# Moving GpSimd's two-input element-wise work to VectorE in a one-core diffusion-transformer kernel

## The chip, the cores and the metric

The kernel runs on one core of one Trainium2 chip. The metric is the device time of one execution in microseconds (us). The core's engines are named as the profile names them: PE (TensorE, matmuls), DVE (VectorE), ACT (ScalarE), POOL (GpSimd) and SP (SyncE, which issues the weight loads). Each engine runs its own queue in order; an instruction whose inputs are not ready holds up what stands behind it on the same engine.

## The reference, cut to what matters

Two blocks work on a latent sequence x of 256 tokens and a context sequence of 256 tokens, both 1024 wide, in float32. The first block has two layers, each a modulated SwiGLU feed-forward, a mixer, and a second feed-forward, with an RMS norm ahead of each:

```python
x = x + 0.5 * mx[:, 2] * swiglu(ada_norm(x, norm_g[l, 0], mx[:, 0], mx[:, 1]), ffn_w_in[l, 0], ffn_w_out[l, 0])
hx = ada_norm(x, norm_g[l, 1], mx[:, 3], mx[:, 4])
# l == 0: even_mixer (differential attention with 2-D rotation, and a bidirectional mLSTM)
# l == 1: odd_mixer (bidirectional gated linear attention)
x = x + mx[:, 5] * yx
x = x + 0.5 * mx[:, 8] * swiglu(ada_norm(x, norm_g[l, 2], mx[:, 6], mx[:, 7]), ffn_w_in[l, 1], ffn_w_out[l, 1])
...
return rms_norm(x, final_g)
```

The second block has two layers of a mixer (latent attention, then neighbourhood attention) and a squared-ReLU MLP, each closed by a layer norm:

```python
h = x * (1 + sc1) + sh1
x = _layer_norm(alpha * x + g1 * y, ln1_g[i], ln1_b[i])
x = _layer_norm(alpha * x + g2 * _mlp(x * (1 + sc2) + sh2, mlp_w1[i], mlp_w2[i]), ln2_g[i], ln2_b[i])
```

## The kernel before

**Tiling.** The activations stay in SBUF, transposed, as `xT`: 8 pieces `k` of 128 channels by 512 tokens, the context (CTX) in columns 0 to 255 and the latent (X) in 256 to 511. Every product of weights and activations is a sum of three matmuls on split numbers (`mm3`): high part by high part (L291), weight high by activation low (L292), weight low by activation high (L293). PE therefore needs a low part of every weight and of every activation.

**Weights.** SP loads a chunk of 128 by 1024 (tile `wraw`, 5 buffers), ACT copies it to the high part (L221, tile `whl`, 4 buffers), and `split_lo` subtracts it from the raw chunk, which gives the low part (L229). Which engine runs L229 stands in `R["lo"]`, set by `lo_on`: VectorE as a rule, and GpSimd (or the two in turn) at the seams between two parts, while the latent MLP's middle runs, and, by the `lo` items, inside the even attention.

**Seams.** Between two parts, `boundary` runs the old part's last output matmuls, the norm and the new part's first matmuls, in a mixture that should keep PE at work. DVE adds each output to `xT` (L811 for an RMS seam, L824 for a layer-norm one), gathers sums (L556, L558), turns PE's token sums into an inverse root by a chain of instructions on two numbers (L526 to L530; for a layer norm also L691 to L696), and writes it on a diagonal (L570). PE spreads the result over the partitions (L571), and DVE then applies the norm for each piece k: L617 and L619 (RMS), or L743, L744, L752 and the low part L753 (layer norm). Before L571 there are no statistics, so nothing of the new part's products can start. At the seam into the last MLP the latent is led instead: L651 and L652 write the scaled, not yet normalised activations, PE multiplies 258 columns of them, and the norm is put in afterwards (L767, L768).

**Attention.** The even attention rotates heads: `stream_shuffle` (L1116), a product with the cosines (DVE) and one with the sines (L1118, POOL), then their sum (L1119). Its steps and those of the gated linear attention run under `in_order`, which binds PE, DVE and ACT, but not POOL, to the order in which the program emits their instructions. Everywhere else a scheduler orders each engine's queue by priorities.

**Other lines of GpSimd.** L686 (low part of the modulated activations, even k), L753 (six of eight k, `LN_LO`), L1705 (two long subtractions for each direction of the gated linear attention), L802 (four additions in the last norm), and memsets and triangular masks.

Of the kernel before, what the change touches and what calls it, by code (L numbers as in the profile page):

```python
# [56 lines left out]
LN_T = ()  # L57
LN_LO = (0, 1, 2, 4, 5, 6)
TMP_BUFS = 9
# [33 lines left out]
def build(nc, tc, ctx, A, stop=None):  # L93
# [9 lines left out]
    V, ACT, PE, G = nc.vector, nc.scalar, nc.tensor, nc.gpsimd  # L103
    POOL = (G,)
    AFTER = (G,)
    EV_LO = (G,)
    RMS_LOS = (G,)
    FN_LOS = (V, G)
    LN_LOS = (G,)
    FULL, CTX, X = slice(0, 512), slice(0, 256), slice(256, 512)  # L110
# [89 lines left out]
    def run_items():  # L200
# [23 lines left out]

        def split_lo(eng=None):
            raw, n, hl = chunks[ws[st["split"]]]
            if eng is None:
                eng = R["lo"][st["split"] % len(R["lo"])]
            eng.tensor_tensor(hl[:, 1, 0:n], raw[:, 0:n], f32(hl[:, 0, 0:n]), ALU.subtract)  # L229
            st["raw"] -= 1  # L230
            st["split"] += 1
            load()
# [23 lines left out]
        for it in items:  # L256
# [13 lines left out]
            elif it[0] == "lo":  # L270
                if half:
                    split_lo(*it[1:])
            elif it[0] == "f":
# [40 lines left out]

    R = {"lo": (V,)}

    def lo_on(*engines):

        R["lo"] = engines

# [357 lines left out]
    def modulate(h, li, shift, scale, s, ks):  # L678
        seg = SEGS[s]
        for k in ks:  # L680
# [4 lines left out]
            V.tensor_scalar(t, x, a, b, ALU.mult, ALU.add)  # L685
            (V if k % 2 else G).tensor_tensor(h.at(1, k, seg), t, f32(h.at(0, k, seg)), ALU.subtract)  # L686

# [11 lines left out]
    class LayerNorm:  # L699
# [39 lines left out]
        def apply(self, s, ks):  # L739
            seg, bc = SEGS[s], self.bc[s]  # L740
            for k in ks:
# [3 lines left out]
                if self.li is not None:  # L745
# [5 lines left out]
                    else:  # L751
                        V.tensor_scalar(t, x, a, b, ALU.mult, ALU.add)  # L752
                    (G if k in LN_LO else V).tensor_tensor(h.at(1, k, seg), t, f32(h.at(0, k, seg)), ALU.subtract)  # L753
            for k in ks:
# [193 lines left out]
    def boundary(exits, norm, entries, e_segs, n_segs, after=()):  # L948
# [10 lines left out]
        if entries and tuple(n_segs) == (1,):  # L959
# [25 lines left out]
            items.extend(("w1", k) for k in keys)  # L985
            do(lo_on, *AFTER)
            do(end_lead, norm)
# [7 lines left out]
        EX = LN_EX if ln else RMS_EX  # L995
        if entries:
            do(lo_on, *(LN_LOS if ln else FN_LOS if isinstance(norm, FinalNorm) else RMS_LOS))
        for u in exits:
# [34 lines left out]
        else:  # L1033
            run_entries(entries, {EN[0]: [soon(norm.stats, 1)], EN[1]: [soon(norm.spread, 1), apply(1, range(8))]})
        do(lo_on, V)


    class Ffn:
# [54 lines left out]
        def middle(self, n_hid, n_out):  # L1093
            for g in range(3):
                for q, u in enumerate(self.hid[g]):
                    if g == 0 and q < (2 if self.seg is FULL else 4):
                        continue
                    body([u], self.seg, n_hid)
                do(lo_on, V)
                do(self.swap)  # L1100
# [6 lines left out]
    def rope(ps, dst, seg):  # L1107
# [4 lines left out]
        if seg.stop == 512:  # L1112
            p = ps[:, 256 - o:512 - o]
            t = tt()
            sh, t1 = t[:, 0:256], t[:, 256:512]
            V.stream_shuffle(sh, p, [(i + 16) % 32 for i in range(32)])  # L1116
            V.tensor_tensor(t1, p, cosT, ALU.mult)
            G.tensor_tensor(sh, sh, sinT, ALU.mult)  # L1118
            V.tensor_tensor(dst[:, X], t1, sh, ALU.add)  # L1119
# [56 lines left out]
    class Even:  # L1176
# [390 lines left out]
        def middle(self):  # L1567
# [49 lines left out]
            def steps():  # L1617
                more(EV_N[0])
                for step in range(21):
# [10 lines left out]
                    if step < 16:  # L1630
                        items.append(("lo", EV_LO[step % len(EV_LO)]))
                    if step in merges:
# [20 lines left out]
    class Odd:  # L1653
# [46 lines left out]
        def decay_log(self, d):  # L1700
# [3 lines left out]
            for o in range(0, 2048, 1024):  # L1704
                G.tensor_tensor(la[:, o:o + 1024], la[:, o:o + 1024], a[:, o:o + 1024], ALU.subtract)  # L1705
            if d:
# [309 lines left out]
    class Out2:  # L2016
# [19 lines left out]
        def middle(self, done=0):  # L2036
            body(self.u[done:3], self.seg)
            if self.seg is X:
                do(lo_on, *POOL)
            body(self.u[3:4], self.seg, hooks={CK: [lambda: center(self.seg, self.rest)]})  # L2040
# [173 lines left out]
    class Mlp:  # L2214
# [39 lines left out]
        def middle(self, n_ada):  # L2254
            for g in range(4):
                for u in self.hid[g][0 if g else 4 if self.seg is FULL else 5:]:
                    body([u], self.seg, n_ada)
                do(lo_on, V)
                do(self.swap)
# [10 lines left out]
    class Na:  # L2270
# [97 lines left out]
        def middle(self):  # L2368
# [17 lines left out]
            def ahead(step):  # L2386
                if 28 <= step < 32:
                    items.extend([("hi",), ("lo", G)])

# [211 lines left out]
```

## Time and profile before

| | |
|---|---|
| median of 3 runs | 2836.68 us (2833.68 to 2838.6) |
| the profiled execution | 2832.91 us |
| its span, first to last instruction | 2831.2 us |
| busy: PE, DVE, ACT, POOL | 2734.7, 2000.6, 1112.1, 240.8 us |
| mean granted TensorE clock | 0.988 |

The span is what the profile shows; the 1.7 us around it are not in any row. A busy figure sums the durations of an engine's instructions; an instruction that stands still while it holds its engine is counted as busy, so a busy DVE is not DVE at work all the time.

### The profile page before, as it was taken

What the parts mean: (1) busy time and instruction counts of PE and PEld (TensorE: products, weight loads), DVE (VectorE), ACT (ScalarE), POOL (GpSimd) and SP (SyncE); (2) the same over time, 40 slices, a digit from 0 to 9 for tenths busy, and PEclk for the clock granted to TensorE, in tenths of its full rate; (3) what the DMA queues carried; (4) which work ended last, traced back from release to release, by engine and by line L of the source; (5) the groups of instructions that cost most, each with busy time, mean ns of one, the idle gap of its engine ahead of it and who ended that gap; (6) DMA issues with size and microseconds to landing.
All of it is one profiled execution on the core that took longest, in us unless ns stands there. A gap on an engine that the chain in (4) does not pass through costs nothing. (4 is left out here: it accounts for less than half of the span.)

```text
span 2831.2 us, 41057 instructions
## 1 busy us (share of the span) xinstructions
PE 2734.7 (97%) x15940; PEld 2363.8 (83%) x15940; DVE 2000.6 (71%) x3817; ACT 1112.1 (39%) x1955; POOL 240.8 (9%) x184
## 2 busy tenths in 40 slices
PE   7999999999999999999999999999999999998998
PEld 4888888878888888888889999976888888976898
DVE  4877786566888787886764755744898857447766
ACT  3222235653222233222264644454443323535544
POOL 0000010221000010000120010200200002003200
PEclk8999999999999999999999999999999999999999
DMA  6656542111566544665542355430165542313453
GB/s 254 203 197 208 179 141 89 48 53 60 191 209 217 170 158 160 214 214 172 170 157 78 113 186 181 133 96 1 60 196 190 180 141 82 121 64 116 144 183 105
DMA packets 114068, 413.15 MB, mean 146 GB/s; under 512 B 12496, under 2 KB 14800, under 8 KB 112336
## 3 DMA queue, kind: packets, MB, share of 16 engines
q1 hardware_dynamic: 112256, 407.64, 44.1%
q10 hardware_dynamic: 1616, 2.88, 0.3%
q8 instruction: 125, 2.05, 0.3%
q14 instruction: 71, 0.58, 0.1%
HBM read 409.42 MB, written 1.05 MB: 145 GB/s over the span
## 5 line engine op out<-in xcount | busy, mean ns | idle before, releaser
L292 PE MATMUL p<-slot,whl 128*128 128x512 f32 (+2 forms) x4256 | 1445.0, 340 | 15.5 <-DVE slot L652 6.1
L291 PE MATMUL p<-slot,whl 128*128 128x512 f32 (+2 forms) x4256 | 1446.0, 342 | 6.8 <-ACT slot L618 2.9
L293 PE MATMUL p<-slot,whl 128*128 128x512 f32 (+2 forms) x4256 | 1441.3, 340 | 6.7 <-DVE whl L229 5.0
L292 PEld LDWEIGHTS p<-slot,whl 128*128 128x128 f32 x4256 | 811.1, 191 | 111.0 <-DVE slot L652 7.1
L291 PEld LDWEIGHTS p<-slot,whl 128*128 128x128 f32 x4256 | 808.0, 191 | 106.0 <-issue 8.6
L293 PEld LDWEIGHTS p<-slot,whl 128*128 128x128 f32 x4256 | 810.9, 191 | 96.0 <-DVE whl L229 5.7
L221 ACT ACTIVATE whl<-wraw 128x1024 fp32r<-128x1024 f32 (+1 forms) x527 | 542.8, 1043 | 510.8 <-PE p L293 290.9
L229 DVE TENSOR_TENSOR whl<-wraw,whl 128x1024 fp32r<-128x1024 f32 (+1 forms) x460 | 560.8, 1221 | 198.8 <-ACT whl L221 190.9
L396 DVE SCALAR_TENSOR_TENSOR t<-wraw,sB 128x1024 bf16<-128x1024 f32 x448 | 534.5, 1218 | 1.8 <-ACT sB L150 1.8
L229 POOL TENSOR_TENSOR whl<-wraw,whl 128x1024 fp32r<-128x1024 f32 (+1 forms) x67 | 167.0, 2499 | 2050.6 <-ACT whl L221 2025.1
L1069 ACT ACTIVATE t<-p 128x512 f32<-128x512 f32 (+1 forms) x86 | 47.1, 548 | 539.5 <-PE p L293 539.5
L1071 DVE TENSOR_TENSOR t<-t,p 128x512 f32<-128x512 f32 (+1 forms) x86 | 53.8, 626 | 218.4 <-PE p L293 161.4
L291 PE MATMUL p<-whl,slot 128*128 128x256 f32 (+1 forms) x432 | 126.3, 292 | 0.0
L292 PE MATMUL p<-whl,slot 128*128 128x256 f32 (+1 forms) x432 | 124.3, 288 | 1.8 <-DVE whl L229 1.8
L293 PE MATMUL p<-whl,slot 128*128 128x256 f32 (+1 forms) x432 | 124.0, 287 | 0.0
L811 DVE SCALAR_TENSOR_TENSOR xT<-p,mod,xT 128x256 f32<-128x256 f32 x192 | 85.8, 477 | 32.3 <-PE p L293 32.1
L590 DVE TENSOR_TENSOR slot<-t,slot 128x512 fp32r<-128x512 f32 (+1 forms) x166 | 101.4, 616 | 3.4 <-ACT slot L589 3.0
L589 ACT ACTIVATE slot<-t 128x512 fp32r<-128x512 f32 (+1 forms) x166 | 89.3, 542 | 18.7 <-DVE t L2239 7.3
L824 DVE SCALAR_TENSOR_TENSOR xT<-p,mod,xT 128x256 f32<-128x256 f32 x119 | 54.3, 478 | 48.9 <-PE p L293 48.5
L556 DVE TENSOR_TENSOR t<-t 128x256 f32<-128x256 f32 (+1 forms) x98 | 74.6, 762 | 19.5 <-ACT t L555 18.4
L291 PEld LDWEIGHTS p<-whl,slot 128*128 128x128 f32 x432 | 83.0, 192 | 4.0 <-issue 2.3
L292 PEld LDWEIGHTS p<-whl,slot 128*128 128x128 f32 x432 | 83.0, 192 | 3.3 <-DVE whl L229 2.2
(314 smaller groups left out, 1959.4 us busy)
## 6 DMA issues: line engine op xcount, KB each, us to landing
wraw<-in_ada SPq DMA_DIRECT2D x224, 512.0 KB, 4.1
wraw<-in_ffn_in SPq DMA_DIRECT2D x176, 512.0 KB, 4.4
wraw<-in_mlp SPq DMA_DIRECT2D x128, 512.0 KB, 3.5
wraw<-in_ffn_out SPq DMA_DIRECT2D x64, 512.0 KB, 4.3
wraw<-in_ffn_out SPq DMA_DIRECT2D x32, 384.0 KB, 3.7
slot<-in_ada SPq DMA_DIRECT2D x8, 1024.0 KB, 16.2
wraw<-in_even_a SPq DMA_DIRECT2D x16, 512.0 KB, 3.5
wraw<-in_odd_a SPq DMA_DIRECT2D x16, 512.0 KB, 3.6
```

What stands on the lines that cost most here:

```text
L221: ACT.activation(out=hl[:, 0, 0:n], in_=raw[:, 0:n], func=AF.Copy)
L229: eng.tensor_tensor(hl[:, 1, 0:n], raw[:, 0:n], f32(hl[:, 0, 0:n]), ALU.subtract)
L291: PE.matmul(ps, w[0], a[0], start=first, stop=False)
L292: PE.matmul(ps, w[0], a[1], start=False, stop=False)
L293: R["pe"] = PE.matmul(ps, w[1], a[0], start=False, stop=last).ins
L396: V.scalar_tensor_tensor(j.bitcast(BF16)[:, 0:1024], raw, 1.0, sB[:, r, :], ALU.mult, ALU.mult, accum_out=mods[li][:, f, r:r + 1])
L556: V.tensor_tensor(a, a, sq[:, seg], ALU.add)
L589: ACT.activation(out=hi, in_=src, func=AF.Copy)
L590: (eng or V).tensor_tensor(lo, src, f32(hi), ALU.subtract)
L811: V.scalar_tensor_tensor(xT[:, m, SEGS[s]], ps[:, q - seg.start:q - seg.start + 256], mod(li, gate)[:, m, s:s + 1], xT[:, m, SEGS[s]], ALU ...
L824: V.scalar_tensor_tensor(xT[:, m, SEGS[s]], ps[:, q - seg.start:q - seg.start + 256], mod(li, gate)[:, m, s:s + 1], xT[:, m, SEGS[s]], ALU ...
L1071: V.tensor_tensor(sa[:, 0:w], sa[:, 0:w], pb, ALU.mult)
```

## The change

All the switches by which an engine is chosen go (`lo_on`, `R["lo"]`, `LN_LO` and the tuples of engines), and five lines always use VectorE:

```diff
-        def split_lo(eng=None):
+        def split_lo():
             raw, n, hl = chunks[ws[st["split"]]]
-            if eng is None:
-                eng = R["lo"][st["split"] % len(R["lo"])]
-            eng.tensor_tensor(hl[:, 1, 0:n], raw[:, 0:n], f32(hl[:, 0, 0:n]), ALU.subtract)
+            V.tensor_tensor(hl[:, 1, 0:n], raw[:, 0:n], f32(hl[:, 0, 0:n]), ALU.subtract)
...
-            (V if k % 2 else G).tensor_tensor(h.at(1, k, seg), t, f32(h.at(0, k, seg)), ALU.subtract)
+            V.tensor_tensor(h.at(1, k, seg), t, f32(h.at(0, k, seg)), ALU.subtract)
...
-                    (G if k in LN_LO else V).tensor_tensor(h.at(1, k, seg), t, f32(h.at(0, k, seg)), ALU.subtract)
+                    V.tensor_tensor(h.at(1, k, seg), t, f32(h.at(0, k, seg)), ALU.subtract)
...
-        if entries:
-            do(lo_on, *(LN_LOS if ln else FN_LOS if isinstance(norm, FinalNorm) else RMS_LOS))
...
-            G.tensor_tensor(sh, sh, sinT, ALU.mult)
+            V.tensor_tensor(sh, sh, sinT, ALU.mult)
...
-                        items.append(("lo", EV_LO[step % len(EV_LO)]))
+                        items.append(("lo",))
...
-                G.tensor_tensor(la[:, o:o + 1024], la[:, o:o + 1024], a[:, o:o + 1024], ALU.subtract)
+                V.tensor_tensor(la[:, o:o + 1024], la[:, o:o + 1024], a[:, o:o + 1024], ALU.subtract)
...
-            if self.seg is X:
-                do(lo_on, *POOL)
```

Of POOL's instructions 122 move: 67 of L229, 30 of L753, 13 of L1118, 8 of L686 and 4 of L1705. The memsets, the masks and the four additions of L802 stay. No DMA is changed, and no matmul is added or removed. The scheduler is given other instructions, so the queues of DVE, ACT and PE shift a little as well.

The rows below are DVE's queue; a number behind a name is that of the buffer or bank. In the changed file the lines stand lower: L220 is the weight's low part (L229 before), L543 and L545 are the sums L556 and L558, L515 to L517 the inverse root's L528 to L530, L557 the diagonal L570, L639 the led low part L652, L678 to L683 the statistics L691 to L696, L730 and L731 the applied norm L743 and L744, L739 and L740 the L752 and L753, and L811 the addition L824.

The first place is the seam from the latent attention into the first MLP, on DVE, where the context's norm is applied (k = 2 to 4) and the latent's statistics begin; before:

```order
L558 TENSOR_TENSOR t_17499<-t_17499,xT_81 128x256
L743 TENSOR_TENSOR xT_81<-xT_81,p_17842 128x256
L753 TENSOR_TENSOR slot_17664<-t_17871,slot_17662 128x256
L744 TENSOR_TENSOR xT_81<-xT_81,p_17842 128x256
L743 TENSOR_TENSOR xT_81<-xT_81,p_17842 128x256
L556 TENSOR_TENSOR t_17500<-t_17500,t_17881 128x256
L752 TENSOR_SCALAR t_17931<-xT_81,mod2_89 128x256
L556 TENSOR_TENSOR t_17500<-t_17500,t_17921 128x256
L744 TENSOR_TENSOR xT_81<-xT_81,p_17842 128x256
L691 TENSOR_SCALAR tiny_18002<-p_17997 128x2
```

and after, at the same place on DVE:

```order
L545 TENSOR_TENSOR t_17499<-t_17499,xT_81 128x256
L740 TENSOR_TENSOR slot_17664<-t_17871,slot_17662 128x256
L543 TENSOR_TENSOR t_17500<-t_17500,t_17881 128x256
L220 TENSOR_TENSOR whl_17889<-wraw_17556,whl_17889 128x1024
L811 SCALAR_TENSOR_TENSOR xT_81<-p_17894,mod2_89,xT_81 128x256
L220 TENSOR_TENSOR whl_17924<-wraw_17614,whl_17924 128x1024
L545 TENSOR_TENSOR t_17499<-t_17499,xT_81 128x256
L543 TENSOR_TENSOR t_17500<-t_17500,t_17921 128x256
L730 TENSOR_TENSOR xT_81<-xT_81,p_17842 128x256
L678 TENSOR_SCALAR tiny_18002<-p_17997 128x2
```

Two subtractions of weights (L220) now stand between the fourth and the fifth piece of the context, ahead of the sums that the latent's statistics need. A third stands between the diagonal (L557) and the first L730 of this seam, and none between the context's token sums and L557.

The second place is the seam into the last MLP, on DVE, where the last outputs come in (L824) and the led low parts (L652) are written; before:

```order
L824 SCALAR_TENSOR_TENSOR xT_81<-p_22853,mod3_90,xT_81 128x256
L652 SCALAR_TENSOR_TENSOR slot_22974<-xT_81,mod3_90,slot_22972 128x256
L558 TENSOR_TENSOR t_22748<-t_22748,xT_81 128x256
L556 TENSOR_TENSOR t_22749<-t_22749,t_22880 128x256
L652 SCALAR_TENSOR_TENSOR slot_22974<-xT_81,mod3_90,slot_22972 128x256 x2
L824 SCALAR_TENSOR_TENSOR xT_81<-p_22888,mod3_90,xT_81 128x256
L652 SCALAR_TENSOR_TENSOR slot_22974<-xT_81,mod3_90,slot_22972 128x256
L558 TENSOR_TENSOR t_22748<-t_22748,xT_81 128x256
```

and after, at the same place on DVE:

```order
L811 SCALAR_TENSOR_TENSOR xT_81<-p_22853,mod3_90,xT_81 128x256
L220 TENSOR_TENSOR whl_22883<-wraw_22653,whl_22883 128x1024
L545 TENSOR_TENSOR t_22748<-t_22748,xT_81 128x256
L543 TENSOR_TENSOR t_22749<-t_22749,t_22880 128x256
L811 SCALAR_TENSOR_TENSOR xT_81<-p_22888,mod3_90,xT_81 128x256
L220 TENSOR_TENSOR whl_22918<-wraw_22758,whl_22918 128x1024
L545 TENSOR_TENSOR t_22748<-t_22748,xT_81 128x256
L543 TENSOR_TENSOR t_22749<-t_22749,t_22915 128x256
L220 TENSOR_TENSOR whl_22953<-wraw_22763,whl_22953 128x1024
L811 SCALAR_TENSOR_TENSOR xT_81<-p_22923,mod3_90,xT_81 128x256
L639 SCALAR_TENSOR_TENSOR slot_22974<-xT_81,mod3_90,slot_22972 128x256
```

Three subtractions of weights have come in between the additions, and the led low parts are pushed behind them.

The third place is the chain of statistics of that same seam on DVE, a few rows on; before:

```order
L652 SCALAR_TENSOR_TENSOR slot_22975<-xT_81,mod3_90,slot_22973 128x256
L691 TENSOR_SCALAR tiny_23070<-p_23065 128x2
L692 TENSOR_SCALAR tiny_23071<-p_23065 128x2
L693 TENSOR_TENSOR tiny_23072<-tiny_23070 128x2
L694 TENSOR_TENSOR tiny_23071<-tiny_23071,tiny_23072 128x2
L526 TENSOR_SCALAR tiny_23073<-tiny_23071 128x2
L528 TENSOR_TENSOR tiny_23078<-tiny_23073 128x2
L529 SCALAR_TENSOR_TENSOR tiny_23079<-tiny_23078,tiny_23071 128x2
```

and after:

```order
L639 SCALAR_TENSOR_TENSOR slot_22975<-xT_81,mod3_90,slot_22973 128x256
L220 TENSOR_TENSOR whl_23035<-wraw_22851,whl_23035 128x1024
L678 TENSOR_SCALAR tiny_23070<-p_23065 128x2
L679 TENSOR_SCALAR tiny_23071<-p_23065 128x2
L680 TENSOR_TENSOR tiny_23072<-tiny_23070 128x2
L681 TENSOR_TENSOR tiny_23071<-tiny_23071,tiny_23072 128x2
L220 TENSOR_TENSOR whl_23091<-wraw_22886,whl_23091 128x1024
L513 TENSOR_SCALAR tiny_23073<-tiny_23071 128x2
L515 TENSOR_TENSOR tiny_23078<-tiny_23073 128x2
```

One subtraction stands ahead of the chain and one in its first half; another follows in its second half and one more between L557 and the first L730.

## Rows read from the trace of the kernel before

**Rows 1.** The page: span, then busy time (share of the span) and instructions of each engine.

```profile
span 2831.2 us, 41057 instructions
...
PE 2734.7 (97%) x15940; PEld 2363.8 (83%) x15940; DVE 2000.6 (71%) x3817; ACT 1112.1 (39%) x1955; POOL 240.8 (9%) x184
```

**Rows 2.** Groups by line and shape, POOL: xcount | busy us, mean ns | idle before, releaser.

```profile
L229 POOL TENSOR_TENSOR whl<-wraw,whl 128x1024 fp32r<-128x1024 f32 x65 | 163.2, 2517 | 2050.6 <-ACT whl L221 2025.1 <-DVE tiny L529 16.3 <-ACT tiny L766 4.5
L753 POOL TENSOR_TENSOR slot<-t,slot 128x256 fp32r<-128x256 f32 x30 | 22.3, 744 | 38.2 <-DVE t L752 24.0 <-ACT slot L748 4.1 <-DVE tiny L694 3.3
L1705 POOL TENSOR_TENSOR slot<-slot 128x1024 f32<-128x1024 f32 x4 | 12.4, 3136 | 25.4 <-ACT slot L1703 25.4
L1118 POOL TENSOR_TENSOR t<-t,cst 128x256 f32<-128x256 f32 x13 | 9.6, 735 | 108.1 <-DVE t L1116 74.0 <-DVE tiny L528 28.9 <-PE p L1542 2.8
...
L229 POOL TENSOR_TENSOR whl<-wraw,whl 128x768 fp32r<-128x768 f32 x2 | 3.8, 1938 | 0.0
```

**Rows 3.** Single lines on DVE: duration ns min/median/max; then idle ahead of L229 (us, times).

```profile
L229 DVE TENSOR_TENSOR whl<-wraw,whl x460: 946/1224/3417, 21.4 to 2808.7; 128x1024 fp32r<-128x1024 f32 x143, 128x768 fp32r<-128x768 f32 x11
...
  ACT whl L221: 190.9, 177
...
L753 DVE TENSOR_TENSOR slot<-t,slot x10: 410/418/2293, 2034.6 to 2642.3; 128x256 fp32r<-128x256 f32 x10
...
L528 DVE TENSOR_TENSOR tiny<-tiny x93: 143/161/2239, 16.6 to 2820.1; 128x2 f32<-128x2 f32 x60, 128x4 f32<-128x4 f32 x33
```

**Rows 4.** Waits of PE: what waited, for whom: us in total, times, longest us.

```profile
PE p L571 <- DVE t L570: 13.9, 10, 4.1
...
PE p L292 <- DVE slot L652: 6.1, 3, 3.7
PE p L293 <- DVE whl L229: 5.0, 2, 3.5
...
PE p L1495 <- DVE tiny L1460: 3.1, 1, 3.1
...
PE p L293 <- POOL whl L229: 1.6, 1, 1.6
```

**Rows 5.** Timeline of the seam into the first MLP: start us, duration us, engine.

```profile
2021.61 2.24 DVE L528 TENSOR_TENSOR tiny<-tiny 128x2 f32<-128x2 f32 x1
...
2021.43 2.40 POOL L229 TENSOR_TENSOR whl<-wraw,whl 128x1024 fp32r<-128x1024 f32 x1 [8.14 <-DVE tiny L529]
...
2027.21 1.90 PE L571 MATMUL p<-t,ones 128*128 128x256 f32 x4 [4.08 <-DVE t L570]
```

**Rows 6.** Timeline of the even attention: DVE and PE.

```profile
620.77 2.22 DVE L528 TENSOR_TENSOR tiny<-tiny 128x4 f32<-128x4 f32 x1
...
624.46 1.06 PE L1495 MATMUL p<-cst,t 128*128 128x128 f32 x4 [3.06 <-DVE tiny L1460]
```

**Rows 7.** Timeline of the first RMS seam: PE.

```profile
404.78 0.67 PE L571 MATMUL p<-t,ones 128*128 128x256 f32 x2 [1.10 <-DVE t L570]
```

**Rows 8.** Timeline of the seam into the last MLP: DVE.

```profile
2594.21 5.90 DVE L846 SCALAR_TENSOR_TENSOR xT<-xT,t 128x256 f32<-128x256 f32 x4 [1.44 <-ACT t L842]
...
2604.18 2.40 DVE L652 SCALAR_TENSOR_TENSOR slot<-xT,mod,slot 128x256 fp32r<-128x256 f32 x1
...
2607.17 2.96 DVE L652 SCALAR_TENSOR_TENSOR slot<-xT,mod,slot 128x256 fp32r<-128x256 f32 x2
...
2612.82 2.23 DVE L558 TENSOR_TENSOR t<-t,xT 128x256 f32<-128x256 f32 x1
2614.97 2.56 DVE L556 TENSOR_TENSOR t<-t 128x256 f32<-128x256 f32 x1
```

**Rows 9.** Stretches: us, busy of each engine (instructions), PEclk, DMA share, GB/s.

```profile
2027.20:2031.00 3.80, 3.79 (x15) 3.45 (x16) 2.90 (x10) 0.83 (x2) 0.18 (x1) 0.55 0.45 138
...
624.40:628.00 3.60, 3.54 (x13) 2.44 (x14) 3.53 (x15) 2.33 (x9) 0.00 (x0) 0.53 0.34 125
...
2611.00:2624.70 13.70, 9.10 (x35) 7.89 (x36) 11.12 (x18) 5.02 (x9) 7.20 (x3) 0.50 0.35 111
```

More of the change, by code (lines that the diff above doesn't have):

```diff
@@ L57 @@
 LN_T = ()
-LN_LO = (0, 1, 2, 4, 5, 6)
 TMP_BUFS = 9
@@ L103, in build @@
     V, ACT, PE, G = nc.vector, nc.scalar, nc.tensor, nc.gpsimd
[L104 to L109, printed above, removed]
     FULL, CTX, X = slice(0, 512), slice(0, 256), slice(256, 512)
@@ L271, in run_items @@
                 if half:
-                    split_lo(*it[1:])
+                    split_lo()
             elif it[0] == "f":
@@ L313, in both @@
             return [self.at(0, k, seg), self.at(1, k, seg)]
-    R = {"lo": (V,)}
-    def lo_on(*engines):
-        R["lo"] = engines
+    R = {}
     def tileA(key, act, kt, cols=128, col=0, order=None):
@@ L985, in boundary @@
             items.extend(("w1", k) for k in keys)
-            do(lo_on, *AFTER)
             do(end_lead, norm)
@@ L1034, in boundary @@
             run_entries(entries, {EN[0]: [soon(norm.stats, 1)], EN[1]: [soon(norm.spread, 1), apply(1, range(8))]})
-        do(lo_on, V)
     class Ffn:
@@ L1098, in middle @@
                     body([u], self.seg, n_hid)
-                do(lo_on, V)
                 do(self.swap)
@@ L2257, in middle @@
                     body([u], self.seg, n_ada)
-                do(lo_on, V)
                 do(self.swap)
@@ L2387, in ahead @@
                 if 28 <= step < 32:
-                    items.extend([("hi",), ("lo", G)])
+                    items.extend([("hi",), ("lo",)])
             def early(step):
```

## The prediction, as it stood before the changed kernel ran

> **What bounds the kernel now.** I read the page's busy line first. PE is busy 2734.7 of 2831.2 us [rows 1], so what an element-wise engine can give or take is only time in which PE stands still or runs slowly, about 96 us of the span plus the stretches at a lower clock. POOL is busy 240.8 us, mostly with the 65 subtractions L229 of 2.517 us each [rows 2]; the same instruction has a median of 1.224 us on DVE, but a maximum of 3.417 us [rows 3].
>
> Second, PE's waits: the list that matters here is for the diagonal L570, 13.9 us in ten waits, for the led low part L652, 6.1 us in three, for low parts of weights, 5.0 us on DVE and 1.6 us on POOL, and for L1460 in the even attention, 3.1 us [rows 4]. Third, the timeline of each such wait. At the seam into the first MLP a DVE instruction on two numbers, L528, lasts 2.24 us, while POOL runs an L229 of 2.40 us that began 0.18 us earlier; the diagonal then comes late, and PE waits 4.08 us [rows 5]. In the even attention L528 lasts 2.22 us in the same way, and PE waits 3.06 us [rows 6]. At the first RMS seam PE waits 1.10 us for the diagonal [rows 7]. At the seam into the last MLP four L846 take 5.90 us, two L652 stretch over 2.40 and 2.96 us, and an L558 over 2.23 us [rows 8]. The usual L528 takes 0.161 us [rows 3]. So DVE instructions with both inputs in SBUF stand still while POOL subtracts. How much DVE time that is in all, no row says; POOL's subtractions and products last 163.2 + 22.3 + 12.4 + 9.6 + 3.8 = 211 us [rows 2], which bounds it from above.
>
> The Trainium skill, "SBUF — State Buffer", section "SBUF: two separate sides", says that a DVE instruction with two SBUF inputs and a GpSimd instruction share a pair of ports as an exclusive lock, held for the whole instruction. By that rule the waiter loses the rest of the other's duration, and 2.24 us beside 2.40 agree; the sum would be the same.
>
> Fourth, the granted clock. After the longest of these waits PE runs at about half speed, the 1.2 GHz level, for a while: 0.55 over 3.80 us after the 4.08 us wait, 0.53 over 3.60 us after the 3.06, and 0.50 over 13.70 us at the last MLP's seam, with 9.10 us of matmuls in it [rows 9]. Each such stretch costs up to half its busy time.
>
> **What the change adds to DVE.** 65 x 1.224 = 79.6 us for L229; 2 shorter ones by 0.946, the shortest on DVE, 1.9; 30 L753 by 0.418, 12.5; four L1705 by the L229 price (same size), 4.9; 13 L1118 and 8 L686 by the L753 price (same size), 8.8: 107.7 us [rows 2, 3]. It takes away the standing still. If about half of the 211 us above is such stand-still, DVE's busy total stays near 2000. What counts is where in DVE's queue the additions land, and each is weighed at its seam. In the plain feed-forward and MLP stages nothing changes, since L229 runs on DVE there already.
>
> **The two layer-norm seams (into the first MLP, into the neighbourhood attention).** Between the context's sums and its diagonal the new queue has no subtraction, so two stand-stills (L528 and, behind it, L696) vanish, the wait of 4.1 us goes, and with it the slow stretch, 3.8 x 0.45 = 1.7 us: 5.8 gained at each [rows 4, 5, 9]. Given back: three subtractions, 3.7 us, now stand between that diagonal and the fifth piece, where before one L753 stood still for 2.293 - 0.418 = 1.9 us; that is 1.8 more, and six L753 on DVE add 6 x 0.418 = 2.5, of which I take 1.0, since DVE partly waits there anyway: 2.8 in all. PE should now wait at L563, the latent's token sums, for L556 behind the two subtractions. Net 3.0 each, **6.0**; between 0 (give-back doubled, to 5.6) and 11.6 (none).
>
> **The RMS seams.** Of the 13.9 us the two waits above are 8.2, which leaves 5.7 in eight; I take the 1.10 us of the first seam for each [rows 4, 7]. Four seams have such a wait, 4.4 us together, and the diagonal is no longer held. Behind it two or three subtractions now stand ahead of the fifth piece's L617 and L619; I take 1.4 us back. **3.0**, between -3 (a new wait of about 2 us at three of them) and 4.4.
>
> **The even attention.** The wait of 3.06 loses L528's 2.22 - 0.16 = 2.06 us [rows 3, 6], and the slow stretch of 3.6 us goes, 3.6 x 0.47 = 1.7 [rows 9]. The two other stops there gain some 0.8 in all by the earlier L1118; one subtraction now stands inside a softmax chain, 1.2 us, in a part that waits for PE. **4.5**, between 1 and 5.5.
>
> **The seam into the last MLP.** PE waits 6.1 us for L652 [rows 4]. Between 2594 and 2617 us six DVE instructions stand still, for about 12.2 us together: at L753's 0.418 for one of this size, two of the four L846 stand for 5.90 - 1.67 = 4.2, two L652 for 2.0 and 2.1, L558 for 1.8, L556 for 2.1 [rows 3, 8]. Six subtractions, 7.3 us, take their place, so the last L652 comes 4.9 us earlier. The 13.70 us at half speed hold 9.10 us of matmuls, of which 4.5 come back [rows 9]. Against it, the statistics' chain gets three subtractions, 3.7 us, in the place of two stand-stills, and I take 1.7 back as a wait at L571. 4.9 + 4.5 - 1.7 = **7.7**, between 0 and 10.6 (6.1 + 4.5).
>
> **Small ones.** From the gated linear attention into its feed-forward: PE's wait of 1.6 for POOL's L229 goes, **1.6**. Into the latent attention: 3.5 of the 5.0 us that PE waits for DVE's L229 is one wait; the subtractions of POOL join the queue ahead of it while L686 no longer stretches, **0.3**, between -1.5 and 1. Start of the odd mixer: two L1705 stand ahead of an L229, **-0.6**, to -2 with a slow stretch. Rotation elsewhere, mask, last norm: 0, covered by PE's work. They cost at most their 13 x 0.42 = 5.5 us if that cover were gone.
>
> **Sum.** 6.0 + 3.0 + 4.5 + 7.7 + 1.6 + 0.3 - 0.6 = 22.5 us. The profiled execution took 2832.91, so 2810.4 for one like it; the median of the three runs is 3.8 higher, 2836.68, and against that I forecast 2836.7 - 22.5 = **2814 us**. All low ends together (0 - 3 + 1 + 0 + 1.6 - 1.5 - 2 = -3.9) give 2841, all high ends (11.6 + 4.4 + 5.5 + 10.6 + 1.6 + 1 - 0.6 = 34.1) 2803.
>
> **Rivals.** *The gain is handed back.* If stand-still and added work are about equal, DVE works as long as before, and every subtraction still ends ahead of a chain somewhere. Then the seams only shift, and only the cleanest places remain (the attention's 3.7), against new waits of the same size: 2833 to 2840, no change. Against it: at the two layer-norm seams the chain ahead of L571 is free of subtractions.
>
> *DVE is blocked at the head of its queue: slower.* A subtraction needs ACT's high part, which needs a free `whl` buffer, which PE frees. On POOL such a wait blocked nobody (POOL was idle 2025.1 us ahead of L229 for it [rows 2]); on DVE the chains and the norm stand behind it. DVE's own L229 already wait 190.9 us in 177 waits, 1.08 us each [rows 3]. If 25 of the 67, about two or three for each of the ten seams and the attention, stand ahead of something that PE needs, and each costs its 1.224 plus 1.08, that is 57.6 us, against 34.7 us of gross gains (11.6 + 4.4 + 5.5 + 10.6 + 1.6 + 1): 2836.7 + 22.9 = 2860. It decides for slower from about 16 such subtractions on. For it: the four subtractions around one chain in the third place of the order. Against it: in most seams the chunk's high part is ready before the sums.
>
> The Trainium skill, "Perfetto Trace Analysis", section "Optimizing Scalar/DVE Operations", says that work of a saturated DVE may be worth moving to Scalar or even GpSimd, though the shared port may spoil that. In the last stretch of [rows 9] DVE is busy 11.12 of 13.70 us, so by the first half of the rule this change goes the wrong way and ends at this rival's 2860; but that busy time holds stand-still, which is the rule's second half.
>
> *The change doesn't do what it says.* Four L802 and the masks stay on POOL, at places where PE hardly waits for DVE: nothing from them.
>
> **Chances.** The forecast 0.52 (2803 to 2826); a half gain, where the last MLP's seam or the layer-norm seams give all back, 0.12 (about 2826); handed back 0.13; slower 0.23, half of it below 2850. The range that leaves out 2 in 10 is 2803 to 2849; the likeliest case's own is 2803 to 2826. A measurement of this kernel tells about 0.2%, 5.7 us, from no change: faster 0.64, same 0.13, slower 0.23.
>
> **What would show it.** Right: no DVE L528 or L696 above 0.3 us; PE's wait for L570 below 6 us in total; the waits for L1460 and L652 below 2 us; a short new wait at L563 in the layer-norm seams; DVE busy near 2000; fewer slow stretches (mean clock above 0.99). Wrong: new PE waits for L753, L619 or L570 above 2 us with DVE standing in front of an L229 until ACT's L221 is through, DVE's idle time for L221 well above 191 us, and slow stretches at the RMS seams.

## Result and profile after

The changed kernel takes 2805.20 us (median of four runs, 2802.59 to 2808.41) against 2836.55 us of the kernel before in the same comparison: ratio 0.9894, 95% interval 0.9882 to 0.9907. The profiled execution took 2802.84 us. The forecast was 2814 us, faster, range 2803 to 2849: the direction is right, and the time lies near the low end of the range. The way there is only partly the one forecast: the gains were larger than their terms, and two losses were not in the sum.

The page of the kernel after, to be read beside [rows 1], gives the span, then busy time, share and instructions of each engine.

```profile
span 2800.8 us, 40932 instructions
...
PE 2723.4 (97%) x15940; PEld 2356.6 (84%) x15940; DVE 1974.1 (70%) x3939; ACT 1114.8 (40%) x1955; POOL 22.1 (1%) x62
```

DVE has 122 instructions more and is busy 26.5 us less. The prediction put the added work at 107.7 us, so by that price about 134 us of DVE's 2000.6 us before were not work. Summed over DVE's instructions that overlap one of POOL's, the time above their usual length (the median of the same line and shape) is 114.1 us before and 0.3 after. This sum is called the overlaps below. POOL falls from 240.8 to 22.1 us. The mean granted clock goes from 0.988 to 0.992.

The weight's low part after, beside [rows 2, 3] (duration ns min/median/max; the last line is idle time of DVE ahead of it):

```profile
L220 DVE TENSOR_TENSOR whl<-wraw,whl x527: 946/1221/1228, 20.9 to 2778.4; 128x1024 fp32r<-128x1024 f32 x166, 128x768 fp32r<-128x768 f32 x10
...
  ACT whl L214: 195.1, 183
```

The maximum is now 1.228 us, where it was 3.417. DVE waits 195.1 us for ACT's high parts, against 190.9: the sign by which the slower rival was to be known, idle time well above 191, is absent from the total.

PE's waits after, beside [rows 4] (in total, times, longest):

```profile
PE p L1952 <- DVE t L1941: 17.5, 17, 2.9
...
PE p L282 <- ACT slot L735: 4.5, 5, 1.4
...
PE p L284 <- DVE whl L220: 3.8, 5, 1.6
...
PE p L282 <- ACT whl L214: 2.2, 1, 2.2
...
PE p L550 <- DVE t L545: 1.2, 3, 0.5
...
PE p L558 <- DVE t L557: 0.9, 1, 0.9
```

The diagonal's waits (now L558 for L557) fall from 13.9 us in ten to 0.9 in one. Those for the led low part and for L1460 are gone. What is new or longer: 17.5 us for the neighbourhood attention's softmax scaling L1941, 4.5 in five for ACT's applied norm L735 (L748 before), and one wait of 2.2 for ACT's high part. The softmax scaling's line in the kernel before was:

```profile
PE p L1970 <- DVE t L1959: 13.0, 16, 2.3
```

To see where the 30.4 us of span went, both traces were laid side by side at the moments at which PE had issued the same matmuls. This table is worked out from the start times of all matmul records; it shows by how many us each stretch became longer (+) or shorter (-). Of PE's 15,940 rows 78 stand at another place in the order than before.

| stretch (us in the trace before) | after | forecast |
|---|---|---|
| start, 0 to 380 | -3.5 | 0 |
| four RMS seams (401, 676, 1030, 1400) | -6.2 | -3.0 |
| even attention (551 to 653) | -3.2 | -4.5 |
| start of the odd mixer (1430 to 1480) | -1.0 | +0.6 |
| gated linear attention to its feed-forward (1620 to 1660) | -2.1 | -1.6 |
| into the latent attention (1790 to 1830) | -4.8 | -0.3 |
| two layer-norm seams (1990 to 2060, 2365 to 2425) | -7.6 | -6.0 |
| start of the neighbourhood attention (2425 to 2480) | **+4.3** | 0 |
| its last steps (2573 to 2590) | **+6.2** | 0 |
| seam into the last MLP (2590 to 2660) | -11.6 | -7.7 |
| all else, each within 0.4 | -1.0 | 0 |

The start's -3.5 is no part of the change: in the experiments below it lies anywhere between -3.7 and +0.7, with the same instructions there. Each column of such a table is one execution. Two other stretches differ between kernels that have the same instructions there: the even attention comes out at -3.2 or -4.7, and the second layer-norm seam at -2.8 to -4.2.

**The layer-norm seam.** The kernel after, at the place of [rows 5], DVE and then PE:

```profile
1999.86 0.16 DVE L515 TENSOR_TENSOR tiny<-tiny 128x2 f32<-128x2 f32 x1
...
2000.66 0.16 DVE L683 TENSOR_TENSOR tiny<-tiny 128x2 f32<-128x2 f32 x1
2000.74 0.87 DVE L557 TENSOR_SCALAR t<-cst,tiny 128x128 f32<-128x128 f32 x4
2001.52 1.22 DVE L220 TENSOR_TENSOR whl<-wraw,whl 128x1024 fp32r<-128x1024 f32 x1
...
2012.63 1.02 PE L550 MATMUL p<-ones,t 128*128 128x1 f32 x8 [0.50 <-DVE t L545]
...
2015.06 0.62 PE L282 MATMUL p<-slot,whl 128*128 128x256 f32 x3 [1.41 <-ACT slot L735]
```

The instruction on two numbers that took 2.24 us takes 0.16, and four diagonals are written in 0.87. The short new wait for the latent's sums is there, 0.50 us. A wait of 1.41 us for ACT's applied norm follows, and the clock falls after it for a while:

```profile
2592.00:2600.00 8.00, 7.16 (x58) 6.95 (x58) 6.63 (x23) 2.82 (x6) 0.00 (x0) 1.00 0.61 200
2551.00:2556.00 5.00, 1.55 (x7) 1.21 (x8) 2.85 (x8) 3.16 (x7) 0.00 (x0) 0.56 0.48 143
...
2015.00:2019.00 4.00, 3.58 (x17) 3.38 (x18) 4.00 (x21) 2.83 (x7) 0.00 (x0) 0.58 0.19 68
```

(Columns as in [rows 9]; the stretches are the seam into the last MLP, the end of the neighbourhood attention and this seam.) The last row, 0.58, is near the 1.2 GHz level, as 0.55 was in [rows 9]: the slow stretch of this seam did not go, it moved behind the next wait.

**The seam into the last MLP.** The kernel after, at the place of [rows 8]:

```profile
2585.25 1.22 DVE L220 TENSOR_TENSOR whl<-wraw,whl 128x1024 fp32r<-128x1024 f32 x1
...
2587.85 2.46 DVE L639 SCALAR_TENSOR_TENSOR slot<-xT,mod,slot 128x256 fp32r<-128x256 f32 x6
...
2600.25 1.13 PE L558 MATMUL p<-t,ones 128*128 128x256 f32 x4 [0.87 <-DVE t L557]
```

Six led low parts take 2.46 us, where one alone took 2.40. PE is busy 7.16 of 8.00 us at full clock (first row of the stretches above), where it had 9.10 of 13.70 us at half.

### The profile page after: what moved, and what is told of

It reads as the page before. It is cut to its first block, busy times and chain, and to the rows that moved or that the text cites. A ratio compares the mean times of both kernels' runs of the same rounds, so it can differ in the third digit from the quotient of the medians.

```text
span 2800.8 us, 40932 instructions
## 1 busy us (share of the span) xinstructions
PE 2723.4 (97%) x15940; PEld 2356.6 (84%) x15940; DVE 1974.1 (70%) x3939; ACT 1114.8 (40%) x1955; POOL 22.1 (1%) x62
## 4 chain that ended last, share of the span: by engine, by line
PE 90%; DVE 6%; ACT 3%; issue 1%; DMA 0%; ACTq 0%; SPq 0%; DVEq 0%
PE p L283 28%; PE p L282 27%; PE p L284 27%; DVE whl L220 1%; PE p L1952 1%; PE p L2137 1%; PE p L2106 1%; PE p L1833 1%; ACT whl L214 1%; PE p L1407 1%; PE p L550 0%; ACT t L1936 0%; PE p L434 0%; PE p L1340 0%; PE p L2111 0%
## 5 line engine op out<-in xcount | busy, mean ns | idle before, releaser
L220 DVE TENSOR_TENSOR whl<-wraw,whl 128x1024 fp32r<-128x1024 f32 (+1 forms) x527 | 633.9, 1205 | 202.5 <-ACT whl L214 195.1
L214 ACT ACTIVATE whl<-wraw 128x1024 fp32r<-128x1024 f32 (+1 forms) x527 | 542.3, 1043 | 511.1 <-PE p L284 300.3
L1052 ACT ACTIVATE t<-p 128x512 f32<-128x512 f32 (+1 forms) x86 | 47.1, 548 | 537.9 <-PE p L284 537.9
L811 DVE SCALAR_TENSOR_TENSOR xT<-p,mod,xT 128x256 f32<-128x256 f32 x119 | 54.1, 479 | 51.7 <-PE p L284 51.3
L282 PEld LDWEIGHTS p<-whl,slot 128*128 128x128 f32 x432 | 82.9, 193 | 3.9 <-issue 2.3
L283 PEld LDWEIGHTS p<-whl,slot 128*128 128x128 f32 x432 | 83.3, 193 | 2.7 <-DVE whl L220 1.6
L284 PEld LDWEIGHTS p<-whl,slot 128*128 128x128 f32 x432 | 83.2, 193 | 0.7
L2218 ACT ACTIVATE t<-p 128x512 f32<-128x512 f32 (+1 forms) x60 | 29.5, 497 | 119.2 <-PE p L284 119.2
## 6 DMA issues: line engine op xcount, KB each, us to landing
slot<-in_ada SPq DMA_DIRECT2D x8, 1024.0 KB, 16.2
```

Source lines behind the costliest of these rows:

```text
L214: ACT.activation(out=hl[:, 0, 0:n], in_=raw[:, 0:n], func=AF.Copy)
L220: V.tensor_tensor(hl[:, 1, 0:n], raw[:, 0:n], f32(hl[:, 0, 0:n]), ALU.subtract)
L282: PE.matmul(ps, w[0], a[0], start=first, stop=False)
L283: PE.matmul(ps, w[0], a[1], start=False, stop=False)
L284: R["pe"] = PE.matmul(ps, w[1], a[0], start=False, stop=last).ins
L811: V.scalar_tensor_tensor(xT[:, m, SEGS[s]], ps[:, q - seg.start:q - seg.start + 256], mod(li, gate)[:, m, s:s + 1], xT[:, m, SEGS[s]], ALU ...
```

## Experiments

Theory A: DVE's instructions stood still while POOL read SBUF, and this stand-still, not the work, was what the change removed. Rival B: the gain comes from where the instructions stand now, that is, from another order on DVE, ACT and PE; then POOL's mere presence costs nothing. A third question is what the two losses in the neighbourhood attention come from.

### The presence of GpSimd alone

Two kernels do all work on DVE as the changed one does, with the same rows in the same order on DVE, PE and ACT. At each of the 67 places where the kernel before subtracted on POOL (`eng` is the engine that it chose), POOL does something useless into a scratch tile, for which no other engine waits. The first takes two inputs from SBUF:

```diff
             V.tensor_tensor(hl[:, 1, 0:n], raw[:, 0:n], f32(hl[:, 0, 0:n]), ALU.subtract)
+            if eng is G:
+                G.tensor_tensor(scr, raw[:, 0:768], f32(hl[:, 0, 0:768]), ALU.subtract)
```

> The changed kernel, and beside each of the 67 weight subtractions that POOL ran before, POOL also subtracts 768 columns of the same chunk into a scratch tile that nobody reads. The queues of DVE, ACT and PE keep the changed kernel's order, row for row. Stand-still theory (DVE instructions with two SBUF inputs stop while POOL subtracts): the useless work, 67 x 1.94 = 130 us of POOL, brings the long L528, L696, L556 and the waits behind them back; most of the 41 us that the seams gained, so 2825 to 2850. Hand-off theory (the gain came from the shorter subtraction, 1.22 in the place of 2.5 us, and from one hand-over less): 2805, within 4 us, since nothing that is needed changes.

Measured: 2869.19 us (2863.43 to 2872.25), ratio to the kernel before 1.0124 (1.0107 to 1.0140); above the range that was expected. POOL's group, then PE's waits, then three DVE lines (min/median/max ns) of this kernel:

```profile
L232 POOL TENSOR_TENSOR scr<-wraw,whl 128x768 f32<-128x768 f32 x67 | 155.7, 2324 | 2241.6 <-ACT whl L222 2206.0 <-issue 35.2
```

```profile
PE p L574 <- DVE t L573: 12.9, 9, 5.0
PE p L296 <- DVE whl L230: 12.5, 12, 2.9
```

```profile
L573 DVE TENSOR_SCALAR t<-cst,tiny x52: 269/279/1922, 18.3 to 2656.9; 128x128 f32<-128x128 f32 x52
...
L230 DVE TENSOR_TENSOR whl<-wraw,whl x527: 947/1221/2903, 21.2 to 2839.2; 128x1024 fp32r<-128x1024 f32 x166, 128x768 fp32r<-128x768 f32 x10
...
L529 DVE TENSOR_SCALAR tiny<-tiny x31: 155/169/1811, 16.3 to 2849.2; 128x2 int32<-128x2 int32 x20, 128x4 int32<-128x4 int32 x11
```

The second takes one input, from the high part only:

```diff
+            if eng is G:
+                G.tensor_scalar(scr, f32(hl[:, 0, 0:768]), 2.0, None, ALU.mult)
```

> As the run before it, but the useless POOL instruction reads one SBUF input (768 columns times two) and writes the scratch. If any POOL instruction that reads SBUF holds DVE's two-input instructions, the time rises in step with this instruction's duration: for 1 to 2 us each, 2815 to 2850. If only POOL's two-input instructions do it, 2805 within 4 us.

Measured: 2822.13 us (2820.49 to 2825.66), ratio 0.9956 (0.9941 to 0.9970): a rise, but a small one beside POOL's 2.66 us each. The same lines:

```profile
L232 POOL TENSOR_SCALAR scr<-whl 128x768 f32<-128x768 f32 x67 | 178.1, 2658 | 2185.5 <-ACT whl L222 2184.0 <-ACT tiny L769 0.7
```

```profile
L573 DVE TENSOR_SCALAR t<-cst,tiny x52: 268/282/923, 18.2 to 2618.7; 128x128 f32<-128x128 f32 x52
...
L230 DVE TENSOR_TENSOR whl<-wraw,whl x527: 944/1222/1846, 21.0 to 2797.9; 128x1024 fp32r<-128x1024 f32 x166, 128x768 fp32r<-128x768 f32 x10
...
L529 DVE TENSOR_SCALAR tiny<-tiny x31: 156/169/790, 16.2 to 2807.8; 128x2 int32<-128x2 int32 x20, 128x4 int32<-128x4 int32 x11
```

Both are against the part of rival B by which POOL's presence costs nothing. With the order unchanged, useless two-input work on POOL costs 64 us over the changed kernel (2869.2 against 2805.2), twice the gain of the change, and DVE's busy time rises by 2050.9 - 1974.1 = 76.8 us with no instruction added to it. PE's waits for the diagonal (L574 for L573 here) are back at 12.9 us. What the end of the stand-still gave in the change itself can't be read from the 64: by the overlaps the stand-still is 79.3 us here and 114.1 in the kernel before, and it falls on other instructions. How much of the 31 us a new order alone would have given, no run separates either. The two-input dummy also holds its `wraw` buffer until POOL is through. That delays loads, but little: SP waits 18.3 us for it in all, and ACT's waits for weight loads rise from 138.6 to 141.2 us.

```profile
SPq L213 <- POOL scr L232: 18.3, 11, 1.7
```

In the one-input kernel POOL is busy longer, 178.1 us, but the largest excess of all three lines is the same 0.62 to 0.64 us, whatever the length of the DVE instruction, and the cost over the changed kernel is 17 us. What a DVE instruction loses is thus not always the rest of POOL's instruction. The Trainium skill, "SBUF — State Buffer", section "SBUF: two separate sides", has the pair of ports held for the whole instruction, whichever engine starts first. For the two-input form the maxima agree with it (1811 - 169 = 1642 ns lost, where POOL's shortest such instruction takes 1802); for the one-input form the runs differ, and there the measurement decides. The trace of the one-input run also tells which part of the instruction holds DVE. POOL, then DVE:

```profile
398.56 2.13 POOL L232 TENSOR_SCALAR scr<-whl 128x768 f32<-128x768 f32 x1 [8.89 <-ACT whl L222]
...
398.60 1.07 DVE L573 TENSOR_SCALAR t<-cst,tiny 128x128 f32<-128x128 f32 x2
...
399.92 1.21 DVE L230 TENSOR_TENSOR whl<-wraw,whl 128x1024 fp32r<-128x1024 f32 x1
```

The two diagonals begin with POOL's instruction and lose 0.6 us; L230 begins 1.36 us into it and loses nothing. Beside all of POOL's instructions that ran in this shortest time, 2.13 us, the five DVE TENSOR_TENSOR with both inputs in SBUF that began in the first 0.3 us were held until about 0.7 us after POOL's start, and of 27 that began from 0.6 us on none lost more than 0.02. Instructions on one tensor and a scalar were held near the end too: the six L573 and L755 that began 1.5 to 1.8 us after POOL's start lost 0.26 to 0.39 us each.

### Which instructions matter

Only the 67 subtractions of weights go to DVE; L753, L686, L1118 and L1705 stay on POOL. Against the kernel before, each tuple of engines for the weights names VectorE, as shown for one:

```diff
-    LN_LOS = (G,)
+    LN_LOS = (V,)
...
-                    items.extend([("hi",), ("lo", G)])
+                    items.extend([("hi",), ("lo",)])
```

> Part of the change alone: every weight subtraction (67) runs on DVE, while the low parts of the norms and the modulation (38), the products of the rotation (13) and the four long subtractions of the gated linear attention stay on POOL. Stand-still theory: the weights' subtractions held 167 of the 219 us that POOL worked on what was moved, so they carry most of the gain; the rest still holds DVE in the layer-norm seams and at the seam into the latent attention: 2808 to 2814, with the latent attention's seam still 2 to 4 us longer than in the changed kernel. Rival (the small products matter as much, for PE waits for them directly): 2818 to 2825.

Measured: 2805.74 us (2804.41 to 2806.17), ratio 0.9899 (0.9884 to 0.9914), the same as the whole change and below the expected range. The complement has the 55 small ones on DVE (the L753 by an empty `LN_LO`) and all weights as before:

```diff
-            (V if k % 2 else G).tensor_tensor(h.at(1, k, seg), t, f32(h.at(0, k, seg)), ALU.subtract)
+            V.tensor_tensor(h.at(1, k, seg), t, f32(h.at(0, k, seg)), ALU.subtract)
...
-            G.tensor_tensor(sh, sh, sinT, ALU.mult)
+            V.tensor_tensor(sh, sh, sinT, ALU.mult)
...
-                G.tensor_tensor(la[:, o:o + 1024], la[:, o:o + 1024], a[:, o:o + 1024], ALU.subtract)
+                V.tensor_tensor(la[:, o:o + 1024], la[:, o:o + 1024], a[:, o:o + 1024], ALU.subtract)
```

> The other part alone: the weights' subtractions stay on POOL where they were, all the smaller ones run on DVE. Stand-still theory: the long holds stay, 2828 to 2835. Rival as above: 2818 to 2825.

Measured: 2841.84 us (2834.85 to 2842.75, eleven runs), ratio 1.0018 (1.0010 to 1.0027); slightly slower, so the expectation missed. Five of the eleven lie at 2834.85 to 2837.82 us and six at 2841.84 to 2842.75, the kernel before at 2830.75 to 2838.72; the trace is of one of the five. A wait of PE in this kernel:

```profile
PE p L571 <- DVE t L570: 13.4, 9, 4.1
```

This wait is 13.9 in [rows 4], and the one for L652 is 6.1 in both kernels. The two on which the forecast stood are all but untouched: they belong to POOL's L229. By the overlaps 97.3 us of stand-still are left in this kernel, and 16.2 in the one with the weights on DVE, of 114.1. By the same side-by-side reading this kernel loses 0.8 and 1.8 us at the layer-norm seams, 2.2 in the last one, and 4.6 at the start of the neighbourhood attention; it gains 1.1 into the latent attention. The kernel with weights alone has 0.0 at the start of the neighbourhood attention and +7.3 at its end. So the two losses have different owners: the first comes with the small ones, the second with the weights.

### The end of the neighbourhood attention

There, under `in_order`, each of the steps 28 to 31 emits a high part for ACT and at once its low part, in the kernel before with `("lo", G)`. After the change DVE meets the low part before ACT has begun the high part. The kernel after, DVE and PE:

```profile
2548.61 1.23 DVE L220 TENSOR_TENSOR whl<-wraw,whl 128x1024 fp32r<-128x1024 f32 x1 [2.84 <-ACT whl L214]
...
2552.87 1.22 DVE L220 TENSOR_TENSOR whl<-wraw,whl 128x1024 fp32r<-128x1024 f32 x1 [1.51 <-ACT whl L214]
...
2551.51 1.05 PE L1952 MATMUL p<-cst,t 128*128 128x128 f32 x4 [2.88 <-DVE t L1941]
...
2555.50 1.09 PE L1952 MATMUL p<-cst,t 128*128 128x128 f32 x4 [2.94 <-DVE t L1941]
```

DVE stands for ACT's L214, the softmax steps L1940 and L1941 stand behind it, PE waits 2.9 us twice, and the clock there is 0.56 (second row of the stretches above). In the kernel before the longest such wait at this place was shorter, though four L1959 stood still beside POOL (1.72 to 2.41 us, 0.48 without it):

```profile
2576.53 0.73 PE L1970 MATMUL p<-cst,t 128*128 128x128 f32 x4 [1.86 <-DVE t L1959]
```

Two remedies. One leaves these four on POOL (the rest as in the changed kernel):

```diff
-                    items.extend([("hi",), ("lo",)])
+                    items.extend([("hi",), ("lo", G)])
```

> The changed kernel, but the four weight subtractions that are written into the last steps of the neighbourhood attention stay on POOL. Between the traces this attention's end is 6.2 us longer after the change. Theory (each of the four stands in program order between two softmax steps on DVE and there waits for ACT's copy): the 6.2 us come back, 2799. Rival (the stretch is only shifted, and the next seam, which waits for DVE anyway, takes it back): 2804 to 2806.

Measured: 2798.21 us (2797.18 to 2801.17), ratio 0.9871 (0.9857 to 0.9886). The other keeps them on DVE, but emits each one attention step after its high part:

```diff
             def ahead(step):
+                if 28 < step < 33:
+                    items.append(("lo",))
                 if 28 <= step < 32:
-                    items.extend([("hi",), ("lo",)])
+                    items.append(("hi",))
```

> The changed kernel, but each of these four subtractions is written one attention step later than its high-part copy, so DVE need not wait for the copy. If DVE's wait for ACT's copy is what costs (its idle time ahead of three of them is 2.84, 1.51 and 1.45 us), 4 to 6 us come back: 2799 to 2801. If the subtraction's own 1.22 us in the softmax chain is what costs, 2804 to 2806.

Measured: 2795.67 us (2795.04 to 2797.12), ratio 0.9861 (0.9847 to 0.9876); more than expected. DVE and PE at this place:

```profile
2548.68 1.22 DVE L220 TENSOR_TENSOR whl<-wraw,whl 128x1024 fp32r<-128x1024 f32 x1
...
2551.30 1.04 PE L1952 MATMUL p<-cst,t 128*128 128x128 f32 x4 [1.76 <-DVE t L1941]
```

The idle time ahead of L220 is gone and the longest PE wait is 1.76. In the side-by-side table the end of the attention goes from +6.2 to 0.0 with POOL and to -0.1 with the shift. The loss was the wait for ACT at the head of DVE's queue, and it is 6.2 us at this place. The seam behind it gains 1.4 us more with either remedy (-13.0 for -11.6).

### The start of the neighbourhood attention, and an attempt at the seam

In the kernel after, PE waits 2.25 us for ACT's high part, and ACT comes to its copies only behind all four pairs of L2274 and L2275 of this piece of work. PE, then ACT:

```profile
2401.05 0.54 PE L282 MATMUL p<-slot,whl 128*128 128x512 f32 x1 [2.25 <-ACT whl L214]
...
2398.49 0.47 ACT L2274 ACTIVATE slot<-p,tiny 128x256 f32<-128x256 f32 x1 [1.31 <-PE p L284]
...
2399.93 3.91 ACT L214 ACTIVATE whl<-wraw 128x1024 fp32r<-128x1024 f32 x4
```

In the kernel before one copy stood in the middle, behind two pairs:

```profile
2425.88 1.07 ACT L221 ACTIVATE whl<-wraw 128x1024 fp32r<-128x1024 f32 x1
```

The next kernel is the shifted one, with the two copies given the scheduler's high priority:

```diff
+EARLY = (("na_a", 12), ("na_a", 13))
...
+            if key in EARLY:
+                with tc.high_priority(AHEAD):
+                    ACT.activation(out=hl[:, 0, 0:n], in_=raw[:, 0:n], func=AF.Copy)
...
```

> The kernel with the four subtractions one step later, and two copies of weights to their high part (ACT) given a higher priority where the neighbourhood attention begins. After the change PE waits there 2.3 us for such a copy, which stands in ACT's queue behind four pairs of outputs, two pairs more than before, and a stretch at half speed follows; the stretch is 4.3 us longer than before. Theory (it is the place in ACT's queue): 4 us come back, 2791 to 2793. Rival (the copy's buffer is not free earlier, so the wait moves onto the outputs behind the copy): 2795 to 2798.

Measured: 2793.31 us (2791.04 to 2796.48), ratio 0.9858 (0.9844 to 0.9871). The two copies run ahead of the pairs:

```profile
2399.03 2.01 ACT L217 ACTIVATE whl<-wraw 128x1024 fp32r<-128x1024 f32 x2 [0.94 <-PE p L289]
```

The +4.3 at this place become 0.0 in the side-by-side table, so the order on ACT was the cause at this place; a rise of 2.4 us, to +2.4, comes back in the stretch behind it (2480 to 2560); there +1.4 stands also in the kernels with the weights alone and with the four on POOL, so it need not be the copies' doing. Against the shifted kernel the median gains 2.4 us with overlapping runs, and the intervals do not tell the two apart. Why the scheduler puts ACT's copies later once the small ones are on DVE, and which of these does it, no run shows.

The last run adds one filling piece to the layer-norm seams (`LN_F = 5` for 4), to cover the wait for L735.

> As the run before it, but at the two layer-norm seams the first five pieces of the context are applied before the latent's sums, not four. In the changed kernel the fifth piece stands behind two weight subtractions in DVE's queue, and PE waits 1.5 us for it and 0.7 us for the latent's sums at each seam. If the fifth piece's place is what costs: 2 to 4 us less than the run before it. If the wait only passes to the latent's sums and to its diagonal: within 1.5 us of it.

Measured: 2796.19 us (2796.03 to 2796.43), ratio 0.9867 (0.9854 to 0.9880): no gain. The median is 2.9 us above the run before it, outside both expectations, though the two profiled executions took the same (2796.43 and 2796.48). The first seam has -2.3 in the place of -3.8, and PE's wait for the applied norm of 1.41 us stands there as before: the wait passes on. The second seam's -4.1 in the place of -2.9 lies within what kernels without this piece show there.

## Where the prediction was right and wrong

**Stand-still and its size: right, too small.** The sum took half of the 211 us as stand-still and expected DVE near 2000 us. It is 1974.1, so the stand-still was some 9 us more by the overlaps above (114.1 for 105.5), and up to 29 more by the busy time. The 211 left out the eight L686 (7.3 us). That POOL's presence alone brings it about is shown by the two-input dummy.

**Layer-norm seams: -7.6 for -6.0, right with one step off.** L528 and the wait at L571 went, and the short wait at the latent's sums came (1.2 us in 3). At the first of the two, 6.1 us were gained by 2032 us of the trace before, where 5.8 were summed; 4.0 were lost again by 2041, where 2.8 were, and 1.5 came back by 2060. The slow stretch was to go with the wait; it came again behind the wait for L735, which was not named.

**RMS seams: -6.2 for -3.0, mis-sized.** I took back 1.4 us for subtractions ahead of the fifth piece. Three seams gave -1.71 to -1.76 each and the last -1.0; no net give-back of that size is seen. At the first seam 1.3 come at the wait itself and 0.4 in the 15 us behind it, for a reason that stays open. The weights alone give the same -6.1.

**Even attention: -3.2 for -4.5.** The wait for L1460 is gone. With the same instructions there, the shifted kernel and the last one give -3.2, the one with the four on POOL and the one with the early copies -4.7, so the term is right within what one execution tells.

**Last MLP seam: -11.6 for -7.7.** The led low parts come at once, as forecast. But all of the 6.1 us of waits went, where the sum took 4.9, and PE's new wait for the diagonal is 0.87 where 1.7 were taken back. With the 4.5 of the slow stretch, which is gone, that makes 9.7; the other 1.9 are not settled.

**Into the latent attention: -4.8 for -0.3, the term that was mis-sized most.** I left PE's wait of 3.5 us as it was, since the subtractions that join the queue were to make up for L686. The rows of the kernel before, which I should have read, DVE, POOL and PE:

```profile
1793.57 1.21 DVE L229 TENSOR_TENSOR whl<-wraw,whl 128x1024 fp32r<-128x1024 f32 x1
...
1796.57 3.25 DVE L685 TENSOR_SCALAR t<-xT,mod 128x256 f32<-128x256 f32 x2
...
1803.67 1.21 DVE L229 TENSOR_TENSOR whl<-wraw,whl 128x1024 fp32r<-128x1024 f32 x1
...
1793.73 1.65 POOL L686 TENSOR_TENSOR slot<-t,slot 128x256 fp32r<-128x256 f32 x1 [1.08 <-DVE t L685]
...
1804.93 0.39 PE L293 MATMUL p<-slot,whl 128*128 128x256 f32 x1 [3.48 <-DVE whl L229]
```

Two L685 took 3.25 us beside POOL, and POOL's L686 took 1.65 beside DVE's L229 at 1793.57; the chain that ended in PE's wait was made of stand-still. In the kernel after two of them take 0.73 us there, and PE does not wait. The weights alone give -3.5, the small ones alone -1.1.

**Odd mixer: -1.0 for +0.6.** No wait came from the two L1705 on DVE; the sign of a small term was wrong.

**Gated linear attention: -2.1 for -1.6.** Right.

**The neighbourhood attention: +10.5, missing.** The words on the kernel before say that the `lo` items are inside the even attention. Four more are in the last steps of the neighbourhood attention (`("lo", G)`), and I overlooked them, so nothing was summed for them. The same passage places another group of L229 in the latent MLP's middle; it is the latent's output projection behind the neighbourhood attention. Neither was looked for in the trace.

**The rivals.** The slower one, a subtraction at the head of DVE's queue, is a real mechanism: it happened at the end of the neighbourhood attention and cost 6.2 us. To decide for slower it needed some 16 such places, and it had four. *Handed back* did not happen at the chains ahead of the diagonals, as argued. *Doesn't do what it says* is out. The first half of the rule of the Trainium skill, "Perfetto Trace Analysis", section "Optimizing Scalar/DVE Operations", that a saturated DVE's work may be moved even to GpSimd, would have given the slower rival's 2860; the runs follow its second half, that the shared port may spoil this.

**On balance.** The named terms sum to -36.5 where 22.5 were forecast, and 10.5 were lost where none was. The two errors, 14.0 and 10.5, went against each other, so the time was met better than the steps, which is luck; of the 9 us by which the forecast is high, 4.5 are the start and the small rest of the table.

## What to carry to other kernels

Before work is put on GpSimd to spare VectorE, or left there, look for VectorE instructions that last longer than their own minimum beside it (min/median/max of a line show them): busy time that is stand-still is no reason to unload. When an instruction is moved to an engine whose queue is bound to program order, its producer has to run one step ahead, or it blocks all that stands behind it; look through every place that emits it, not only the seams. A table of both traces at equal PE work finds gains and losses that no list of waits adds up.

## What the runs showed of the hardware

- The stand-still is mutual. POOL's L686 took 1.65 us beside DVE's L229 and 0.84 to 0.85 at the next ones in that stretch, and the useless 768-column subtraction has a mean of 2324 ns beside the work on DVE, its shortest 1802.
- It is not confined to DVE instructions with both inputs in SBUF, as the prediction had it: the diagonals (L573, a tensor with scalars) and integer instructions on two numbers (L529) were held as well, up to 1.64 us. An instruction with a PSUM operand was not: in the first RMS seam of the kernel before three L617 ran in their usual time beside POOL's subtraction.

```profile
405.49 1.27 DVE L617 SCALAR_TENSOR_TENSOR t<-xT,mod,p 128x256 f32<-128x256 f32 x3
...
404.85 2.40 POOL L229 TENSOR_TENSOR whl<-wraw,whl 128x1024 fp32r<-128x1024 f32 x1 [0.50 <-ACT whl L221]
```

- A one-input POOL instruction of 2.66 us on the mean held a DVE instruction of the three lines for at most 0.64 us, a two-input one for up to 1.64 to 1.68 us, near its shortest time of 1.80. Where it ran in its shortest time, 2.13 us, the one-input instruction held two-input DVE instructions in its first 0.7 us only.
